# The pool of the expert tables' staging tiles moves from right behind h^T to the top of SBUF

## The chip, the cores and the metric

The kernel runs on one core of one Trainium2 chip. The metric is the device time of one execution in microseconds: the median of three runs is 1944.34 us (1943.15 to 1944.63). The profile shown below is of one further execution.

## The reference

256 tokens of width 1024 pass through two residual layers, all in float32. Layer 0 mixes the tokens with gated DeltaNet heads and block attention, layer 1 with latent attention. After each mixer stands the PEER feed-forward layer, which takes most of the time: 8 heads choose 16 of 16384 single-neuron experts for each token, and

```
act = gelu(einsum('td,ted->te', h, u[expert]))
out = einsum('te,ted->td', gates * act, v[expert])
```

Here `h` is the normalised and modulated activation, `u` and `v` are two tables of 16384 x 1024 in each layer.

## The kernel before

**No gather.** The kernel doesn't fetch the chosen experts. It multiplies h with the whole table u, weighs the result by a matrix of gates that is zero where an expert wasn't chosen, and multiplies that by the whole table v. Each table comes in 128 slabs of 128 experts (512 KB each) per layer.

**Two numbers for one.** A float32 value is split in a rounded part hi and a rest lo (`split`, line 131: ScalarE writes hi with a cast, VectorE writes lo with a subtraction). A product of two such values is three TensorE products: hi by hi, hi by lo, lo by hi.

**A matmul has two operands in SBUF.** The stationary one (128 x 128) is loaded into the array by an LDWEIGHTS, the moving one (256 or 512 columns) then streams through it. The profile shows the first as PEld, the second as PE, and names them in the order moving, stationary: `ps<-hT,hi` has hT as moving operand and hi as stationary one. Each matmul has its own LDWEIGHTS, which runs beside the matmul ahead of it.

**The stages of one layer's experts.** The u stage (`u_slab`, lines 619 to 628) loads a slab of u into `raw` (3 buffers), splits it into `hi` and `lo` (2 buffers each), and issues 24 matmuls of 256 columns: 16 of line 626 (8 k-tiles of hi as stationary operand, each with both parts of h^T moving) and 8 of line 628 (lo with the first part of h^T). Beside it VectorE selects the experts (`choose`) in the first half, and builds the gate matrix (`g_batch`, lines 639 to 653) in the second. The v stage (`v_pair`, line 783) loads a slab of v into the same `raw`, splits it into the same `hi` and `lo`, and issues 12 matmuls of 512 columns with hi or lo moving; the stationary operand is the weighted activation, split into `whi` and `wlo` of the pool `oh`. The last six slabs of a layer have lines of their own (736).

**Other products.** The projections (lines 135 to 137) go by weights that are loaded to `wraw` and split into `whi` and `wlo` of the pool `wp`, which lies at the right end of SBUF; the PEER queries (`queries`) are such products with h^T moving and the weights stationary, 48 of 256 columns for each of six groups in a layer. Line 323 (`two_tiles`) has weights moving and h^T stationary; these weights lie in several pools, and those of the first queries in `hi` and `lo` among others.

**What orders the work.** Tile pools are stacks that grow from the left or the right end of a partition's bytes. `hp` (h^T) and `st` (`raw`, `hi`, `lo`) are opened first and stay open to the end; the pools of the stages are opened and closed above them. All table and weight transfers are issued by SyncE, and wait there for a buffer.

Of the kernel before, what the change touches and what calls it, by code (L numbers as in the profile page):

```python
# [67 lines left out]
class Trunk:  # L68
# [222 lines left out]
    def tail(self, products, add, nxt, tmp):  # L291


        def run(g):
            for _ in g:
                pass
        run(products(0, 0))
        run(products(0, 1))
        run(add(0, 0))
        run(add(0, 1))  # L300
        nxt.norm(0)
        run(products(1, 0))
        p = products(1, 1)
        next(p)
        squares = add(1, 0)
        next(squares)
        nxt.turn(0)
        run(p)
        nxt.make(0, tmp, squares)
        run(add(1, 1))  # L310
# [1330 lines left out]
    def run(self, out):  # L1641
        nc = self.nc
        self.hp = self.ctx.enter_context(self.pool("h"))
        self.st = self.ctx.enter_context(self.pool("st"))
        right, late = ExitStack(), ExitStack()
        self.order = ExitStack()
        start = ExitStack()
# [243 lines left out]
```

## Time and profile before

| | |
|---|---|
| median of the runs | 1944.34 us |
| the profiled execution's own time | 1942.01 us |
| its span, first to last instruction | 1940.2 us |
| granted TensorE clock, mean share | 0.999 |
| TensorE busy | 1908.1 us (98%) |
| weight loads busy | 1753.0 us (90%) |
| VectorE busy | 1534.9 us (79%) |
| ScalarE busy | 952.7 us (49%) |
| the core's 16 DMA engines busy | 57.4% |

TensorE is busy almost throughout, so the time goes by what TensorE does and how fast. The busy share says nothing on that speed: matmuls overlap, and one that takes longer from start to start looks just as busy. So a matmul's pace is read from the starts of two matmuls and the count between them.

### The profile page before, as it was taken

Reading aid. Unit: us, or ns where it says so; the run is one execution under the profiler, and the core shown is the slowest. Engines: PE = TensorE matmul, PEld = TensorE weight load, DVE = VectorE, ACT = ScalarE, POOL = GpSimd, SP = SyncE. Lnnn points to the kernel's source line nnn. Section 1 sums busy time; section 2 is a strip of 40 time slices with the busy share of each in tenths; the row PEclk is TensorE's granted clock in tenths of the full one; section 3 lists DMA queues with packets and bytes.
Section 4 is the critical chain, followed back from the end, with each engine's and each line's share of the span. In section 5 each row is a group of like instructions: output and inputs, shape, how many; then the busy total and the mean of one; then the engine's idle time right before and its main releaser. Section 6 shows DMA issues by size and latency. Waiting matters only on the chain.

```text
span 1940.2 us, 36008 instructions
## 1 busy us (share of the span) xinstructions
PE 1908.1 (98%) x14368; PEld 1753.0 (90%) x14368; DVE 1534.9 (79%) x3265; ACT 952.7 (49%) x1309; POOL 49.9 (3%) x131
## 2 busy tenths in 40 slices
PE   6999999999999999999999999999999999999998
PEld 6999999999999888888889899999999988888886
DVE  7879699989977789877657668898777778985565
ACT  3866545454344444445546664545444444444453
POOL 7000000000000000000000000000000000000000
PEclk9999999999999999999999999999999999999999
DMA  7557485558645555589743454555545555556673
GB/s 319 177 172 250 187 275 179 185 187 291 229 164 167 172 175 174 178 286 331 229 129 115 163 218 169 183 187 178 171 164 169 168 174 175 173 176 204 192 224 106
DMA packets 97080, 376.67 MB, mean 194 GB/s; under 512 B 11920, under 2 KB 12176, under 8 KB 90256
## 3 DMA queue, kind: packets, MB, share of 16 engines
q1 hardware_dynamic: 96912, 374.37, 57.4%
q8 instruction: 112, 1.84, 0.4%
q14 instruction: 56, 0.46, 0.1%
HBM read 373.28 MB, written 1.05 MB: 193 GB/s over the span
## 4 chain that ended last, share of the span: by engine, by line
PE 88%; DVE 4%; DMA 3%; ACT 2%; issue 1%; SPq 0%; ACTq 0%; DVEq 0%
PE ps L783 31%; PE ps L626 26%; PE ps L628 13%; PE ps L649 3%; PE ps L135 3%; PE ps L136 3%; PE ps L137 3%; DMA raw<-in_v_dram 2%; PE ps L736 1%; PE ps L323 1%; DVE wlo L131 1%; PE ps L1207 1%; DMA wraw<-in_w_dram 1%; PE ps L946 1%; PE ps L456 1%
## 5 line engine op out<-in xcount | busy, mean ns | idle before, releaser
L131 ACT CAST hi<-raw 128x1024 fp32r<-128x1024 f32 x508 | 533.6, 1051 | 772.6 <-PE ps L626 385.4
L131 DVE TENSOR_TENSOR lo<-raw,hi 128x1024 fp32r<-128x1024 f32 x508 | 619.8, 1221 | 260.7 <-ACT hi L131 256.7
L626 PE MATMUL ps<-hT,hi 128*128 128x256 f32 x4096 | 538.3, 284 | 0.0
L626 PEld LDWEIGHTS ps<-hT,hi 128*128 128x128 f32 x4096 | 509.0, 192 | 0.0
L628 PE MATMUL ps<-hT,lo 128*128 128x256 f32 x2048 | 287.2, 283 | 0.0
L783 PE MATMUL ps<-hi,whi 128*128 128x512 f32 x976 | 266.4, 394 | 2.0 <-ACT hi L131 1.9
L628 PEld LDWEIGHTS ps<-hT,lo 128*128 128x128 f32 x2048 | 264.2, 192 | 0.0
L783 PE MATMUL ps<-hi,wlo 128*128 128x512 f32 x976 | 261.3, 389 | 0.0
L783 PE MATMUL ps<-lo,whi 128*128 128x512 f32 x976 | 261.2, 389 | 0.0
L783 PEld LDWEIGHTS ps<-hi,wlo 128*128 128x128 f32 x976 | 183.2, 188 | 38.8
L783 PEld LDWEIGHTS ps<-lo,whi 128*128 128x128 f32 x976 | 183.1, 188 | 38.9 <-DVE lo L131 0.2
L783 PEld LDWEIGHTS ps<-hi,whi 128*128 128x128 f32 x976 | 180.1, 188 | 39.3 <-ACT hi L131 4.5
L131 DVE TENSOR_TENSOR wlo<-wraw,whi 128x1024 fp32r<-128x1024 f32 (+1 forms) x84 | 98.7, 1200 | 41.0 <-ACT whi L131 41.0
L131 ACT CAST whi<-wraw 128x1024 fp32r<-128x1024 f32 (+1 forms) x84 | 83.7, 1031 | 30.7 <-PE ps L137 9.3
L645 DVE TENSOR_TENSOR ohG<-ohB,t 128x512 f16<-128x512 f16 x256 | 98.6, 416 | 0.0
L135 PE MATMUL ps<-hT,whi 128*128 128x256 f32 x288 | 84.0, 292 | 7.7 <-ACT hT L246 7.1
L639 DVE TENSOR_TENSOR ohA<-t,t 128x1024 f16<-128x1024 f16 x128 | 87.3, 682 | 0.0
L136 PE MATMUL ps<-hT,whi 128*128 128x256 f32 x288 | 82.1, 285 | 0.2 <-DVE hT L250 0.2
L137 PE MATMUL ps<-hT,wlo 128*128 128x256 f32 x288 | 82.2, 286 | 0.0
L649 PE MATMUL ps<-ohG,ohA 128*128 128x64 f16 x2048 | 78.6, 193 | 0.0
L649 PEld LDWEIGHTS <-ohA 128*128 128x128 f16 x2048 | 67.0, 97 | 12.1 <-issue 8.5
L353 DVE SCALAR_TENSOR_TENSOR t<-t 128x1024 f32<-128x1024 f32 x56 | 67.4, 1219 | 12.6 <-DMA t<-in_modT_dram 9.5
(480 smaller groups left out, 2254.6 us busy)
## 6 DMA issues: line engine op xcount, KB each, us to landing
raw<-in_uT_dram SPq DMA_DIRECT2D x256, 512.0 KB, 3.3
raw<-in_v_dram SPq DMA_DIRECT2D x256, 512.0 KB, 3.8
t<-in_modT_dram SPq DMA_DIRECT2D x56, 512.0 KB, 5.3
wraw<-in_w_dram SPq DMA_DIRECT2D x13, 1024.0 KB, 5.9
raw<-in_modT_dram SPq DMA_DIRECT2D x24, 512.0 KB, 4.4
wraw<-in_wq_dram SPq DMA_DIRECT2D x12, 1024.0 KB, 5.9
mw<-in_mod_dram SPq DMA_DIRECT2D x8, 1024.0 KB, 13.8
wraw<-in_w0start_dram SPq DMA_DIRECT2D x4, 1024.0 KB, 12.0
```

Source lines behind the costliest of these rows:

```text
L131: return self.nc.scalar.copy(hi, src), self.nc.vector.tensor_sub(lo, src, hi.bitcast(F32))
L135: mm(out, l[0], r[0], start=start, stop=False)
L136: mm(out, l[0], r[1], start=False, stop=False)
L137: mm(out, l[1], r[0], start=False, stop=stop)
L323: mm(ps[g][:, i], e.hT[:, s, k, sl], w[:, b, k, :], start=s + k + b == 0, stop=s == 1 and n == KD - 1)
L353: self.nc.vector.scalar_tensor_tensor(w, w, 1.0, row, op0=OP.mult, op1=OP.mult, accum_out=self.modc[layer][:, c:c + 1])
L626: mm(pair, hi[:, k], hT[:, s, k], start=k == 0 and s == 0, stop=False)
L628: mm(pair, lo[:, k], hT[:, 0, k], start=False, stop=k == KD - 1)
L639: nc.vector.tensor_tensor(A, self.iota_t[:, None].to_broadcast(full), pairs(0, full), op=OP.is_equal)
L645: nc.vector.tensor_tensor(B[:, j], b0, pairs(2 + j, part), op=OP.mult)
L649: nc.tensor.matmul(ps[:, t], A[:, t // 2, :, t % 2], B[:, j, t // 2, :, t % 2], start=j == 0, stop=j == 1)
L783: self.nc.tensor.matmul(acc[i][c], w[a][:, j, i * P:(i + 1) * P], v[b][:, c * 512:(c + 1) * 512], start=first and j + a + b == 0, stop=False)
```

## The change

One argument is added: the pool `st` is taken from the right end of SBUF.

```diff
         self.hp = self.ctx.enter_context(self.pool("h"))
-        self.st = self.ctx.enter_context(self.pool("st"))
+        self.st = self.ctx.enter_context(self.pool("st", side="right"))
         right, late = ExitStack(), ExitStack()
```

In the two programs as they are built every engine has the same instructions in the same order with the same waits. Only addresses differ. The pools behind `st` on the left move down by its 28672 bytes, those at the right end move down by as much to make room, and `st` itself moves up by 170304 bytes. The start of the tiles that the text speaks of, in bytes of a partition, with the remainder by 512:

| tile | before | rem. | after | rem. |
|---|---|---|---|---|
| hT (pool h) | 13984 | 160 | 13984 | 160 |
| raw (st), the first of 3 | 30368 | 160 | 200672 | 480 |
| lo (st) | 42656, 46752 | 160 | 212960, 217056 | 480 |
| hi (st) | 50848, 54944 | 160 | 221152, 225248 | 480 |
| whi, wlo of the v stage (oh), layer 0 | 84128 to 92320 | 160 | 55456 to 63648 | 160 |
| whi, wlo of the v stage (oh), layer 1 | 71840 to 80032 | 160 | 43168 to 51360 | 160 |
| wraw, whi, wlo of the projections (wp) | 163808 to 229344 | 480 | 135136 to 200672 | 480 |
| ckT, cqT, in layer 1's mixer | 67264, 71360 | 192 | 38592, 42688 | 192 |
| dead and qkT, in layer 0's mixer | 77472 on, 93856 | 160 | 48800 on, 65184 | 160 |

Slices within these tiles begin at multiples of 512 bytes from their start, so the remainder of a tile is that of each of its matmul operands.

## Rows read from the trace of the kernel before

**Rows 1.** The page: busy time by engine, and the chain by line.
```profile
PE 1908.1 (98%) x14368; PEld 1753.0 (90%) x14368; DVE 1534.9 (79%) x3265; ACT 952.7 (49%) x1309; POOL 49.9 (3%) x131
...
PE ps L783 31%; PE ps L626 26%; PE ps L628 13%; PE ps L649 3%; PE ps L135 3%; PE ps L136 3%; PE ps L137 3%; DMA raw<-in_v_dram 2%; PE ps L736 1%; PE ps L323 1%; DVE wlo L131 1%; PE ps L1207 1%; DMA wraw<-in_w_dram 1%; PE ps L946 1%; PE ps L456 1%
```
**Rows 2.** Stretches: start:end length, busy PE PEld DVE ACT POOL, PEclk, DMA, GB/s.
```profile
261.00:648.00 387.00, 387.00 (x3591) 385.71 (x3590) 338.01 (x861) 178.46 (x206) 1.53 (x1) 1.00 0.61 203
648.00:830.00 182.00, 182.00 (x1239) 149.88 (x1239) 156.60 (x268) 80.16 (x92) 0.00 (x0) 1.00 0.55 175
...
1175.00:1562.00 387.00, 387.00 (x3591) 385.71 (x3590) 314.99 (x805) 173.96 (x202) 1.53 (x1) 1.00 0.52 172
```
**Rows 3.** The chain in order of time: start us, us, what.
```profile
264.36 1.92 PE ps L626 x16
267.24 1.92 PE ps L626 x16
...
1744.07 113.47 PE ps L783 x500
```
**Rows 4.** Lines 626 and 628: count, ns min/median/max, first and last start.
```profile
L626 PEld LDWEIGHTS ps<-hT,hi x4096: 187/192/192, 261.2 to 1561.6; 128*128 128x128 f32 x196
L626 PE MATMUL ps<-hT,hi x4096: 278/283/365, 261.2 to 1561.7; 128*128 128x256 f32 x196
...
L628 PE MATMUL ps<-hT,lo x2048: 279/283/283, 263.2 to 1562.6; 128*128 128x256 f32 x187
```
**Rows 5.** Line 135 with h^T moving, the same view.
```profile
L135 PEld LDWEIGHTS ps<-hT,whi x288: 186/188/333, 22.6 to 1171.8; 128*128 128x128 f32 x144
L135 PE MATMUL ps<-hT,whi x288: 276/276/583, 22.6 to 1171.9; 128*128 128x256 f32 x144
```
**Rows 6.** Timeline of PE in two query groups: start us, us, instruction.
```profile
226.10 0.28 PE L136 MATMUL ps<-hT,whi 128*128 128x256 f32 x1
...
231.40 0.28 PE L136 MATMUL ps<-hT,whi 128*128 128x256 f32 x1
...
1160.81 0.28 PE L135 MATMUL ps<-hT,whi 128*128 128x256 f32 x1
...
1165.57 0.28 PE L135 MATMUL ps<-hT,whi 128*128 128x256 f32 x1
```
**Rows 7.** Line 323, view as in rows 4: moving operand in st, wp, ckT.
```profile
L323 PE MATMUL ps<-hi,hT x64: 276/283/387, 206.3 to 1133.6; 128*128 128x256 f32 x64
...
L323 PE MATMUL ps<-whi,hT x64: 278/279/386, 1019.9 to 1033.2; 128*128 128x256 f32 x64
...
L323 PE MATMUL ps<-ckT,hT x8: 277/278/281, 1121.1 to 1130.0; 128*128 128x256 f32 x8
```
**Rows 8.** Timeline of PE, products of 512 columns in the projections.
```profile
181.75 0.40 PE L136 MATMUL ps<-wlo,qkT 128*128 128x512 f32 x1
...
191.37 0.39 PE L136 MATMUL ps<-wlo,qkT 128*128 128x512 f32 x1
...
1102.73 0.40 PE L135 MATMUL ps<-whi,cqT 128*128 128x512 f32 x1
...
1104.60 0.40 PE L137 MATMUL ps<-whi,cqT 128*128 128x512 f32 x1
```
**Rows 9.** Stretches of layer 0's u stage, columns as in rows 2.
```profile
350.00:400.00 50.00, 50.00 (x419) 50.00 (x419) 47.54 (x217) 22.80 (x26) 0.00 (x0) 1.00 0.55 181
452.00:500.00 48.00, 48.00 (x504) 47.67 (x503) 47.42 (x88) 19.56 (x24) 0.00 (x0) 1.00 0.84 284
```
**Rows 10.** Groups by shape: busy, mean ns | idle before, releasers.
```profile
L131 DVE TENSOR_TENSOR lo<-raw,hi 128x1024 fp32r<-128x1024 f32 x508 | 619.8, 1221 | 260.7 <-ACT hi L131 256.7 <-PE ps L783 1.6
...
L131 DVE TENSOR_TENSOR wlo<-wraw,whi 128x1024 fp32r<-128x1024 f32 x80 | 96.2, 1225 | 41.0 <-ACT whi L131 41.0
```
**Rows 11.** DMA issues: form, count, KB each, median us to landing.
```profile
raw<-in_v_dram SPq DMA_DIRECT2D x256, 512.0 KB, 3.8
...
wraw<-in_w1out_dram SPq DMA_DIRECT2D x4, 1024.0 KB, 4.8
```

## The prediction

> **What bounds the kernel now.** I read the page first: TensorE is busy 98% of the span, and the chain that ended last runs through it: line 783 (v stage) 31%, lines 626 and 628 (u stage) 39% [rows 1]. [...] So an edit pays there only if it changes the pace of the matmuls or if another engine falls behind TensorE. The program's order and waits are unchanged, so the question is whether pace depends on where operands lie. The busy time can't say that. The start times can.
>
> The pace of the u stage: the 16 matmuls of line 626 begin at 264.36 and, one slab later, at 267.24, so 24 matmuls take 2.88 us, 120.0 ns each [rows 3]. Nearly all are alike: line 628 has a minimum of 279 and a median of 283 ns [rows 4]. The same form, h^T moving over 256 columns and a 128 x 128 weight tile standing, is found in the query groups. There 42 steps from 1160.81 to 1165.57 take 4.76 us, 113.3 ns each, and 45 steps from 226.10 to 231.40 take 5.30 us, 117.8 ns each [rows 6]. By start times, 9 of the 12 groups (6 a layer) have the first pace and 3 the second; none has 120. The single durations agree: a load of 192 ns and a matmul of 283 in the u stage [rows 4], 188 and 276 at line 135 [rows 5].
>
> What differs? Not the moving tile (h^T in both), the columns or the clock. By the table of addresses, the u stage's two operands have the same remainder by 512 (160 and 160), those of the query groups don't (160 and 480). Line 323 separates this from the loop: one loop, h^T standing, weights moving from several pools. From hi (remainder 160, equal to h^T's) the median is 283, from whi (480) 279, from ckT (192) 278 [rows 7]. ckT starts at byte 67264 and hi at 50848, h^T at 13984, so ckT isn't much farther from h^T than hi is: I take it that the low address bits count, equal ones costing about 7 ns a matmul, and not the distance. Whether 512 is the period or 128 or 256 the rows can't tell; 160 and 480 differ by all three.
>
> **The change, part by part.** Only `st` changes its remainder, from 160 to 480. All other moved tiles go down by 28672 bytes, 56 times 512.
>
> U stage. Matmuls: 4096 + 2048 = 6144 [rows 4], all from equal remainders to unequal ones, 160 moving against 480 standing, exactly the query groups' case. Value taken: the groups' mean, (9 x 113.3 + 3 x 117.8) / 12 = 114.4 ns, 5.6 less than 120.0: 34.4 us. Bounds: 6.7 x 6144 = 41.2 if all go at 113.3, 2.2 x 6144 = 13.5 if all go at 117.8, and 0 if the addresses aren't the reason.
>
> V stage. Here hi and lo move and whi and wlo stand. Now both have remainder 160; later 480 against 160. Matmuls: 122 slabs x 12 x 2 layers = 2928. Pace now: 500 in 113.47 us, 226.9 ns [rows 3]. Nearest row for 480 against 160 at 512 columns: 42 steps from 181.75 to 191.37, 9.62 us, 229.0 ns [rows 8]. So this stage loses: 2.1 x 2928 = 6.1 us. Bounds: 8 steps from 1102.73 to 1104.60, 1.87 us, 233.8 ns (480 against 192) [rows 8], which would be +6.9 x 2928 = 20.2 us; below nothing, the 256-column products' fall of 6.7 ns, a gain of 19.6 us. No 512-column row shows that, so I take the nearest one.
>
> What is late next. In layer 0's u stage VectorE is busy 338.01 of 387.00 us [rows 2], but 47.54 of 50 in one stretch and 47.42 of 48 in another [rows 9]. At 114.4 ns the first needs 47.7 us of TensorE, just enough cover. In the second, VectorE lets no more than 0.6 us go of some 2. With what is lost around single slabs I take 3 us off the gain, between 0 and 8; the 8 is half of layer 0's 17.2. Layer 1 has 314.99 of 387 [rows 2] and loses nothing.
>
> Splits and transfers. A VectorE subtraction in `st` takes 1221 ns, one in `wp`, which ends where `st` will end, 1225 [rows 10]: 4 ns, off the chain. A slab lands in 3.8 us for 512 KB, a weight tile at the right end in 4.8 for 1024 KB [rows 11], so nothing there is slower by the byte; counted as 0, and the casts too. The 64 matmuls of line 323 with hi moving gain 4 ns each, 0.3 us, counted as 0.
>
> Sum: -34.4 + 6.1 + 3 = -25.3 us. The profiled execution took 1942.0 us, so 1916.7; the median of the runs is 2.3 above that execution, which gives **1919.0 us**.
>
> [...]
>
> **The rivals.**
> *The addresses don't matter.* The 120.0 could come from the u loop's order (16 of hi, then 8 of lo), and the 113.3 from the projections' order of three. For it: both paces, 113.3 and 117.8, occur in one piece of code, so something besides the address sets the pace. Against it: line 323 has one order and three durations. The changed kernel would then be the old one: 1944.3 us. [...]
> *Slower: the v stage pays more than the u stage gets.* V's matmuls go to 233.8 ns, +20.2 us, while u only reaches 117.8, -13.5: +6.7, or 1951 us. With the u pace unchanged and v at 229.0 it is +6.1, or 1950. It decides once v's loss per matmul exceeds 2.1 times u's gain per matmul (6144 / 2928). For it: both 512-column stretches with unequal remainders are above 226.9 [rows 8]. Against it: the row nearest in operands asks for 2.1 ns only.
> *VectorE takes over.* If layer 0's u stage gains nothing, -17.2 + 6.1 = -11.1, or 1933 us. For it, 47.42 of 48; against it, 338 of 387 for the whole.
>
> **How the numbers follow.** Forecast 0.74, VectorE 0.04, no effect 0.13, slower 0.09. The forecast's own range: u all at 113.3 with v unchanged, -41.2 + 3 = -38, 1906; u all at 117.8 with v at 229.0, -7.4, 1937. To hold 8 in 10 I go up to 1945, which takes in the case without effect, and down to 1904, for no loss at VectorE: 1904 to 1945. Bounds for a measurable change are 0.2%, 3.9 us: faster 0.78 (forecast and VectorE), same 0.13, slower 0.09.
>
> **What would show it.** Right: lines 626 and 628 with medians of about 188 (load) and 276 to 281 (matmul), a slab every 2.72 to 2.83 us, both u stages some 370 us long; line 783 at about 229 ns from start to start; subtractions at 1221 and landings at 3.8 unchanged. Wrong: u still at 2.88 us a slab (no effect of addresses); v over 232 ns; or TensorE waiting for `lo` through layer 0's u stage, which would put the bound on VectorE.

## The result and the profile after

The changed kernel takes 1918.45 us (median of 4 executions, 1916.8 to 1922.05), the kernel before 1944.49 beside it: ratio 0.987, 95% interval 0.9853 to 0.9887, so 26.0 us less. The forecast was 1919.0.

The profiled execution took 1922.05 us, the slowest of the four, while that of the kernel before (1942.01) lies under all its other ones (1943.15 to 1944.75). The two traces are therefore only 19.9 us apart (spans of 1940.2 and 1920.3), and it is these 19.9 us that can be laid out stage by stage.

The page after, busy time by engine and the chain by engine; it answers to [rows 1]:

```profile
PE 1881.9 (98%) x14368; PEld 1717.7 (89%) x14368; DVE 1533.5 (80%) x3265; ACT 951.6 (50%) x1309; POOL 49.6 (3%) x131
...
PE 78%; DVE 10%; DMA 7%; ACT 3%; issue 2%; SPq 0%; ACTq 0%; DVEq 0%
```

TensorE still is busy 98% of the span, with 26.2 us less of it and as many instructions. The stages are read from the first and last start of a line, one layer at a time. Lines 626 (u) and 783 (v) of the kernel before, layer 0 then layer 1 (count, ns min/median/max, first and last start):

```profile
L626 PE MATMUL ps<-hT,hi x2048: 278/283/365, 261.2 to 647.5; 128*128 128x256 f32 x187
...
L626 PE MATMUL ps<-hT,hi x2048: 278/283/365, 1175.5 to 1561.7; 128*128 128x256 f32 x187
...
L783 PE MATMUL ps<-hi,whi x488: 388/389/504, 648.5 to 999.2; 128*128 128x512 f32 x163
...
L783 PE MATMUL ps<-hi,whi x488: 388/389/499, 1562.8 to 1911.7; 128*128 128x512 f32 x163
```

The same rows of the changed kernel:

```profile
L626 PE MATMUL ps<-hT,hi x2048: 276/276/384, 261.5 to 635.6; 128*128 128x256 f32 x187
...
L626 PE MATMUL ps<-hT,hi x2048: 276/276/369, 1170.4 to 1538.9; 128*128 128x256 f32 x187
...
L783 PE MATMUL ps<-hi,whi x488: 387/392/505, 636.6 to 993.8; 128*128 128x512 f32 x163
...
L783 PE MATMUL ps<-hi,whi x488: 388/392/505, 1539.9 to 1891.5; 128*128 128x512 f32 x163
```

| stage, first to last start | before | after | difference |
|---|---|---|---|
| u, layer 0 | 386.3 | 374.1 | -12.2 |
| u, layer 1 | 386.2 | 368.5 | -17.7 |
| v, layer 0 | 350.7 | 357.2 | +6.5 |
| v, layer 1 | 348.9 | 351.6 | +2.7 |

Their sum is -20.7 us; what lies ahead, between and behind is 0.8 longer. The two u stages, alike before, differ by 5.6 us after.

The pace shows in the chain of the changed kernel in order of time (start us, us, what), as in [rows 3]:

```profile
328.32 1.81 PE ps L626 x16
331.05 1.81 PE ps L626 x16
...
1722.41 103.56 PE ps L783 x452
```

A slab of 24 matmuls comes every 2.73 us, 113.8 ns each; it was 2.88 and 120.0. In the v stage 103.56 / 452 is 229.1 ns against 226.9. The single durations of lines 626 and 323 after (they answer to [rows 4] and [rows 7]):

```profile
L626 PEld LDWEIGHTS ps<-hT,hi x4096: 186/188/192, 261.4 to 1538.8; 128*128 128x128 f32 x196
L626 PE MATMUL ps<-hT,hi x4096: 276/276/384, 261.5 to 1538.9; 128*128 128x256 f32 x196
```

```profile
L323 PE MATMUL ps<-hi,hT x64: 276/279/392, 206.5 to 1128.6; 128*128 128x256 f32 x64
...
L323 PE MATMUL ps<-dead,hT x48: 277/280/289, 206.8 to 219.6; 128*128 128x256 f32 x48
...
L323 PE MATMUL ps<-ckT,hT x8: 280/280/284, 1116.1 to 1124.9; 128*128 128x256 f32 x8
```

Load 188 and matmul 276 ns are those of line 135 in [rows 5]. VectorE's subtraction is as before (1221 ns in [rows 10]), and a v slab lands in 3.7 us (3.8 in [rows 11]):

```profile
L131 DVE TENSOR_TENSOR lo<-raw,hi 128x1024 fp32r<-128x1024 f32 x508 | 619.4, 1221 | 239.6 <-ACT hi L131 235.7 <-issue 0.2
```

```profile
raw<-in_v_dram SPq DMA_DIRECT2D x256, 512.0 KB, 3.7
```

### The profile page after: what moved, and what is told of

Read it like the earlier page. It is cut to its first block, busy times and chain, and to the rows that moved or that the text cites. A ratio compares the mean times of both kernels' runs of the same rounds, so it can differ in the third digit from the quotient of the medians.

```text
span 1920.3 us, 36008 instructions
## 1 busy us (share of the span) xinstructions
PE 1881.9 (98%) x14368; PEld 1717.7 (89%) x14368; DVE 1533.5 (80%) x3265; ACT 951.6 (50%) x1309; POOL 49.6 (3%) x131
## 3 DMA queue, kind: packets, MB, share of 16 engines
HBM read 373.28 MB, written 1.05 MB: 195 GB/s over the span
## 4 chain that ended last, share of the span: by engine, by line
PE 78%; DVE 10%; DMA 7%; ACT 3%; issue 2%; SPq 0%; ACTq 0%; DVEq 0%
PE ps L783 28%; PE ps L626 21%; PE ps L628 10%; PE ps L649 3%; PE ps L135 3%; PE ps L137 3%; DVE lo L131 3%; PE ps L136 3%; DMA raw<-in_v_dram 3%; DMA t<-in_modT_dram 2%; PE ps L736 1%; PE ps L323 1%; DVE wlo L131 1%; PE ps L1207 1%; ACT hi L131 1%
## 5 line engine op out<-in xcount | busy, mean ns | idle before, releaser
L131 DVE TENSOR_TENSOR lo<-raw,hi 128x1024 fp32r<-128x1024 f32 x508 | 619.4, 1221 | 239.6 <-ACT hi L131 235.7
L626 PE MATMUL ps<-hT,hi 128*128 128x256 f32 x4096 | 514.3, 278 | 1.7 <-ACT hi L131 1.7
L626 PEld LDWEIGHTS ps<-hT,hi 128*128 128x128 f32 x4096 | 485.8, 188 | 1.9 <-ACT hi L131 1.9
L628 PE MATMUL ps<-hT,lo 128*128 128x256 f32 x2048 | 276.3, 277 | 1.5 <-DVE lo L131 1.4
L628 PEld LDWEIGHTS ps<-hT,lo 128*128 128x128 f32 x2048 | 252.4, 188 | 2.9 <-DVE lo L131 2.7
L649 PEld LDWEIGHTS <-ohA 128*128 128x128 f16 x2048 | 67.3, 97 | 12.2 <-issue 8.9
```

The costliest lines, as they stand in the source:

```text
L131: return self.nc.scalar.copy(hi, src), self.nc.vector.tensor_sub(lo, src, hi.bitcast(F32))
L626: mm(pair, hi[:, k], hT[:, s, k], start=k == 0 and s == 0, stop=False)
L628: mm(pair, lo[:, k], hT[:, 0, k], start=False, stop=k == KD - 1)
L649: nc.tensor.matmul(ps[:, t], A[:, t // 2, :, t % 2], B[:, j, t // 2, :, t % 2], start=j == 0, stop=j == 1)
```

## The experiments

Theory: the pace of TensorE follows the low bits of the moving operand's address against those of the standing one. Main rival: it is the place, `st` far from h^T or in the upper part of SBUF. All kernels but one compute the same, with the same instructions; they differ in unused bytes ahead of a pool or tile, with further ones behind it so that the other tiles keep their remainders. Each ratio is to the kernel before on the same chip, whose median was 1944.49 us beside the changed kernel and 1945.6 to 1946.2 us beside the others.

In the table the distance is the standing operand's remainder less the moving one's, by 256. The paces are the mean steps between matmul starts over both layers, in the one trace of each kernel; steps over 130 ns (u) or 250 ns (v) are left out, since those hold waits or other work.

| kernel | st at | u: distance, ns | v: distance, ns | time, us | ratio, interval |
|---|---|---|---|---|---|
| before | left, 160 | 0, 120.0 | 0, 227.3 | | 1 |
| after | top, 480 | 64, 114.0 | 192, 229.1 | 1918.45 | 0.987 (0.9853 to 0.9887) |
| top_equal | top, 160 | 0, 120.0 | 0, 227.3 | 1945.07 | 0.9997 (0.9987 to 1.0007) |
| left_unequal | left, 480 | 64, 114.0 | 192, 229.0 | 1919.61 | 0.9867 (0.985 to 0.9883) |
| h_too (h^T at 480) | top, 480 | 0, 120.0 | 192, 229.0 | 1953.26 | 1.0041 (1.0028 to 1.0053) |
| d256 | top, 416 | 0, 120.0 | 0, 227.3 | 1945.62 | 0.9997 (0.9988 to 1.0007) |
| d128 | top, 288 | 128, 118.9 | 128, 233.0 | 1953.45 | 1.004 (1.0025 to 1.0055) |
| d32 | top, 192 | 32, 118.3 | 224, 233.3 | 1950.76 | 1.0017 (1.0006 to 1.0027) |
| d192 | top, 96 | 192, 117.0 | 64, 233.3 | 1940.8 | 0.9982 (0.997 to 0.9993) |
| v_equal | top, 480 | 64, 115.7 | 0, 227.3 | 1924.39 | 0.9893 (0.9877 to 0.991) |
| oh_early | top, 480 | 64, 116.0 | 192, 229.2 | 1931.19 | 0.9927 (0.9911 to 0.9944) |
| v_only | top, 480 | 64, 113.9 | 0, 227.2 | 1915.9 | 0.9839 (0.9823 to 0.9854) |
| d96_v | top, 256 | 96, 118.2 | 0, 227.3 | 1936.57 | 0.9949 (0.993 to 0.9969) |
| light | top, 480 | 64, 114.0 | 192, 229.0 | 1919.22 | 0.9864 (0.9848 to 0.9881) |

**Place or low bits.** First the move without the new remainder, then the new remainder without the move (both edits against the changed kernel).

```diff
+        self.t(self.ctx.enter_context(self.pool("gap", side="right")), [P, 80])
         self.st = self.ctx.enter_context(self.pool("st", side="right"))
+        self.t(self.ctx.enter_context(self.pool("gap2", side="right")), [P, 48])
```

> The pool st stays at the top of SBUF, but 320 bytes lower, so that hi and lo have h^T's remainder by 512 again (160 and 160); 192 further bytes below it keep every other tile's remainder. Theory of the low address bits: lines 626 and 628 back at 120.0 ns from start to start (load 192, matmul 283), line 783 back at 227.2; time 1940 to 1945 us. Rival, it is the place (the distance from h^T, or the upper part of SBUF): 114.1 and 229.1 ns as in the changed kernel; 1917 to 1922 us.

```diff
-        self.st = self.ctx.enter_context(self.pool("st", side="right"))
+        self.t(self.ctx.enter_context(self.pool("gap")), [P, 80])
+        self.st = self.ctx.enter_context(self.pool("st"))
+        self.t(self.ctx.enter_context(self.pool("gap2")), [P, 48])
```

> The pool st lies behind h^T as before the change, but 320 bytes further, so that hi and lo have remainder 480 against h^T's 160; 192 further bytes behind it keep the other tiles' remainders. Theory of the low address bits: u stage at 114.1 ns, line 783 at 229.1, so the time of the changed kernel without any move to the top: 1917 to 1922 us. Rival, it is the place: 120.0 and 227.2 ns; 1942 to 1946 us.

The low bits carry all of it: the move alone brings nothing (0.9997), the 320 bytes alone bring the whole gain (0.9867). One slab of top_equal in the chain, at 1.92 us for 16 as before:

```profile
331.40 1.92 PE ps L626 x16
333.32 0.96 PE ps L628 x8
```

Line 626 of left_unequal, with the durations of the changed kernel:

```profile
L626 PE MATMUL ps<-hT,hi x4096: 276/276/387, 260.4 to 1535.1; 128*128 128x256 f32 x196
```

**Equality or a good value.** h^T is moved by 320 bytes too.

```diff
+        self.t(self.ctx.enter_context(self.pool("gaph")), [P, 80])
         self.hp = self.ctx.enter_context(self.pool("h"))
+        self.t(self.ctx.enter_context(self.pool("gaph2")), [P, 48])
```

> The changed kernel with the pool of h^T 320 bytes further and 192 bytes behind it: h^T has remainder 480, hi and lo 480; whi and wlo of the v stage keep 160. Theory that equal remainders count and not the particular value: u stage back at 120.0 ns with line 783 still at 229.1, so 1947 to 1952 us, slower than before. Rival, 480 is a good remainder for a standing tile and 160 a bad one: u stage at 114.1, 1917 to 1922 us.

Equality: 480 against 480 is at 120.0 ns again, and the v stage's loss is left (229.0 ns). The time, 1953.26 us, is 1.3 over the expected range, which left out one thing that the trace shows: with h^T at 480 the query groups' operands are equal too, since their weights lie at 480. All 12 groups now have a mean step of 119.7 to 120.0 ns, where the kernel before has 113.4 to 117.8, an estimated 3 us for their 576 matmuls. So the effect also appears in matmuls that have no operand in `st`. Line 626 and a v piece of h_too (112.72 / 492 = 229.1 ns), and between them line 135, which had a median of 276 ns in [rows 5]:

```profile
L626 PE MATMUL ps<-hT,hi x4096: 278/283/366, 264.1 to 1569.6; 128*128 128x256 f32 x196
```

```profile
L135 PE MATMUL ps<-hT,whi x288: 277/283/582, 22.6 to 1179.7; 128*128 128x256 f32 x144
```

```profile
1753.22 112.72 PE ps L783 x492
```

**The period, and what lies within it.** The edit is top_equal's, with gaps of 64, 192, 288 and 384 bytes.

> The pool st at the top with remainder 416 (64 bytes lower than in the changed kernel), which is 256 from h^T's 160 and from that of whi and wlo. If the period of the effect is 512: u stage near 114 ns, 1917 to 1922 us. If it is 256, 128 or 64: u stage at 120.0 ns as for equal remainders, line 783 at 227.2, 1940 to 1945 us. If it is the place and no remainder: 114.1 and 229.1, 1917 to 1922 us.

> The pool st at the top with remainder 288: 128 from h^T's 160 and from that of whi and wlo, in the other direction than 480 (192 from it). If the period is 256 (416 was as slow as equal, 480 not): u stage faster than 120.0 ns, at 113 to 118, time 1915 to 1935 us. If the period is 128: 120.0 and 227.2 ns, 1942 to 1948 us.

> The pool st at the top with remainder 192, 32 from h^T's 160. If any difference inside the period gives the faster pace: u stage at 113 to 118 ns, 1915 to 1935 us. If operands that fall into the same 64 or 128 bytes behave as equal ones: 120.0 ns, 1942 to 1948 us.

> The pool st at the top with remainder 96, 64 below h^T's 160 instead of 64 above it (by 256). Theory that only the size of the distance counts: u stage at 113 to 114.5 ns, line 783 at 229, so the changed kernel's 1917 to 1922 us. Rival, the sign counts (standing ahead of moving is another case than behind it, so what is good for the u stage is bad for the v stage): u stage at 117 to 120 ns, 1930 to 1950 us.

At 256 bytes (d256) u and v have the paces of equal operands, 120.0 and 227.3 ns, at 128 (d128) they don't, 118.9 and 233.0: the period is 256, as far as the distances tried tell. Within it no simple rule came out. For the u stage 32, 96 and 128 bring 1 to 2 ns only (118.3, 118.2 and 118.9), 64 brings 6 (114.0). The expectation of d192 that only the size of the distance counts fell: 64 below h^T (192 by 256) gives 117.0 ns in the u stage where 64 above gives 114.0, and in the v stage 64 gives 233.3 and 192 gives 229.1. The 117.0 is a mix, though: d192 starts both u stages at 113.3 ns, the pace of distance 64, and goes over to 117.8 after 20 and 23 slabs for good. Its traced execution is also one of three at 1945.66 to 1946.38 us; the other seven took 1939.12 to 1940.88, so there the mix may be another. All unequal distances tried cost the v stage something (229.0 to 233.3 ns against 227.3). These pieces show an equal pair, d256 (227.0 ns), and an unequal one, d32 (233.5):

```profile
1750.91 99.87 PE ps L783 x440
```

```profile
1750.32 173.70 PE ps L783 x744
```

The times expected of d32 and d128 (under 1935 us if the u stage got faster) left the v stage out and were missed. The two kernels are the forecast's slower rival come true: with d128 the u stage gets 1.1 x 6144 = 6.8 us and the v stage pays 5.7 x 2928 = 16.7, 9.9 more in all; measured are 7.6 (1953.45 against 1945.83). The times of top_equal and d256 lie 0.1 and 0.6 us over their ranges.

**A version with both stages at their best, and what spoilt the first try.** With the whole pool `oh` moved:

```diff
         oh = left.enter_context(self.pool(f"oh{layer}"))
         a1 = left.enter_context(self.pool(f"act1_{layer}"))
         act1 = self.act_tiles(a1)
+        self.t(oh, [P, 80])
```

> The changed kernel with 320 bytes ahead of the tiles of the pool oh, so that whi and wlo of the v stage have remainder 480, like hi and lo, while h^T against hi and lo stays unequal. Theory of the low address bits, with equal ones better at 512 columns: u stage unchanged at 114.1 ns, line 783 from 229.1 to 227.2; 1.9 x 2928 = 5.6 us less than the changed kernel, 1912 to 1914 us. Rival, the v stage's pace comes from the place of hi and lo at the top or from VectorE and the transfers: line 783 stays at 229.1, 1917 to 1922 us.

The v stage did what was expected (227.3 ns). The time did not fall (1924.39 us), because the second half of both u stages, where line 649 runs between the slabs, slowed down (0.94 us for eight matmuls of line 628 at 1402.49 us, 0.91 in the changed kernel at 1403.89). The next two runs part the tiles that had moved together: v_only puts the 320 bytes ahead of whi and wlo alone, oh_early ahead of ohA, ohB and ohG alone (and of the index tile that VectorE builds them from).

```diff
         accs = [[self.ps("o") for _ in range(2)] for _ in range(TT)]
+        self.t(oh, [P, 80])
...
+        self.t(oh, [P, 48])
         mods, ready = after()
```

> The changed kernel, in which only whi and wlo of the v stage go to remainder 480 (320 bytes ahead of them, 192 behind); the tiles of line 649 and the gelu's results keep 160, unlike in the run v_equal. Theory, the v stage's pace follows the remainders and the u stage's second half was spoilt in v_equal by the other tiles that moved with the pool oh: u stage at 113 to 114 ns in both halves, line 783 at 227.2, so 5.6 us under the changed kernel: 1911 to 1915 us. Rival, whi and wlo themselves or chance spoilt the u stage in v_equal (117.8 ns in the second half of the stage): 1922 to 1926 us as there.

> The changed kernel in which only the tiles of line 649 (ohA, ohB, ohG) go from remainder 160 to 480; whi, wlo and the gelu's results keep 160. Theory, the short matmuls of line 649 decide in which of its two paces the u stage goes on: the second half of both u stages at 117 to 118 ns instead of 113.4 as in v_equal, line 783 at 229.1, so 8 us over the changed kernel: 1925 to 1929 us. Rival, the gelu's result tiles did it in v_equal (they had moved too): u stage at 113.4 in the second half, 1917 to 1921 us.

The tiles of line 649 did it: 1931.19 us in oh_early, 1915.9 in v_only. In v_equal and oh_early the second half is at the slower pace, some 117.8 ns, in both layers, in the changed kernel, left_unequal, v_only and light mostly at the faster one, some 113.4, in both. The pace depends on how much of line 649 ran just ahead. In layer 1's second half of the changed kernel, the second slab behind 16 of its matmuls is at the faster pace, 1.81 us for 16 of line 626, and the second slab behind 32, two batches in a row, at the slower one:

```profile
1437.62 0.50 PE ps L649 x16
...
1440.92 1.81 PE ps L626 x16
...
1443.64 0.98 PE ps L649 x32
...
1447.53 1.89 PE ps L626 x16
```

In oh_early, with h^T, hi and lo at the same addresses, it is the other way round:

```profile
1444.55 0.50 PE ps L649 x16
...
1447.96 1.89 PE ps L626 x16
...
1450.79 0.98 PE ps L649 x32
...
1454.60 1.81 PE ps L626 x16
```

Behind 16 matmuls of line 649 the changed kernel, left_unequal, v_only and light go on at the faster pace in 27 or 28 of a layer's 28 places, v_equal and oh_early at the slower one in 24 to 27. The time of oh_early is 2.2 us over its range; its layer 0 also has a slower first half (115.5 against 114.2 ns, 1.3 x 1536 = 2.0 us), which the next lines show.

So for one pair of remainders the u stage has two paces, some 113.4 and 117.8 ns, and stays in one for many slabs (up to 33 in the changed kernel). In these traces a change from one slab to the next stands at an interruption: a step of over 200 ns, or matmuls of line 609 or 649 in between. In layer 1 all six kernels with distance 64 change at the same four of the first 61 slabs (23, 30, 53 and 60, counted from 0), so these changes are not chance. The addresses alone don't settle it: oh_early has the changed kernel's operand addresses all through layer 0's first half, yet it began that stage in the second pace (a slab every 2.83 us from 266.54 on), in which it stayed for some 30 slabs:

```profile
266.54 1.88 PE ps L626 x16
268.43 0.94 PE ps L628 x8
269.37 1.89 PE ps L626 x16
```

In the changed kernel the second pace follows on one disturbed piece (1.05 us for eight matmuls):

```profile
404.84 1.81 PE ps L626 x16
406.65 1.05 PE ps L628 x8
407.70 1.88 PE ps L626 x16
```

v_only beats the kernel before clearly. Against the changed kernel it was not timed directly: its ratio is 0.0031 lower, 6 us, where the v stage's 1.9 x 2928 = 5.6 were expected; the intervals (0.9823 to 0.9854 and 0.9853 to 0.9887) just overlap, so the step from one to the other is likely, but not shown by the times. Its 1915.9 us is 0.9 over the expected range. Its v piece (102.58 / 452 = 226.9 ns):

```profile
1714.34 102.58 PE ps L785 x452
```

The last run looked for a better distance for the u stage and found none (118.2 ns and 1936.57 us at 96):

> A search for a version better than v_only (1915.9 us): st at remainder 256, 96 from h^T's 160, and whi and wlo of the v stage at 256 too, as equal as in v_only. The v stage is expected at 227.2 ns by all theories. For the u stage the runs so far have 120.0 ns at distance 0, 118.3 at 32, 113.4 (second pace 117.8) at 64 and 119.0 at 128. If 64 is the bottom of a valley between 32 and 128: 116 to 118.5 ns at 96, 6144 times 2 to 4.5 ns over v_only, 1928 to 1943 us. If the pace falls on beyond 64: under 113.4 ns, under 1912 us.

**VectorE in layer 0's u stage.** The 32 modulation tiles are cut:

```diff
-                    self.mod_tile(layer, c, w, row)
+                    self.mod_tile(layer, c, *(x[:, :8 if (layer, p) in ((0, 5), (1, 0), (1, 1), (1, 2)) else D] for x in (w, row)))
```

> The changed kernel in which the 32 modulation tiles (line 353) that VectorE works off in layer 0's u stage are summed over 8 of their 1024 columns; the rest of that sum is left out, their transfers stay. Theory, VectorE holds TensorE back in layer 0's u stage: that stage (first to last slab) goes from 372.4 us to layer 1's 366.8 or a little less, so 4 to 6 us under the changed kernel: 1912 to 1915 us, with no TensorE wait for lo. Rival, the transfers are late there (DMA share 0.82 between 450 and 500 us): the stage stays at 371 to 373, the time at 1917 to 1921 us.

Weight loads of the changed kernel in layer 0's u stage (columns: busy us, mean ns, idle before us and releaser):

```profile
L626 PEld LDWEIGHTS ps<-hT,hi 128*128 128x128 f32 x2048 | 242.9, 188 | 1.9 <-ACT hi L131 1.9
L628 PEld LDWEIGHTS ps<-hT,lo 128*128 128x128 f32 x1020 | 125.8, 188 | 2.8 <-DVE lo L131 2.7
```

and of light, with the first and last start of line 626 in that stage:

```profile
L626 PEld LDWEIGHTS ps<-hT,hi 128*128 128x128 f32 x2048 | 242.9, 188 | 1.4 <-ACT hi L131 1.3
L628 PEld LDWEIGHTS ps<-hT,lo 128*128 128x128 f32 x1024 | 126.2, 188 | 0.1
```

```profile
L626 PE MATMUL ps<-hT,hi x2048: 276/276/385, 264.5 to 634.6; 128*128 128x256 f32 x187
```

The wait for lo is gone, and the stage takes 370.1 us in place of 374.1; layer 1's takes 368.5. (The expectation counts from slab to slab, 1.7 less for each stage.) So by these two traces VectorE costs 4.0 of the 5.6 us; the stage takes 373.1 to 374.6 us in the three kernels that have this work and the same paces (the changed kernel, left_unequal and v_only). The remaining 1.6 is above all a wait for the cast of hi (1.3 us idle in light), which stands behind a transfer of the conditioning vector, as the chain of light has it:

```profile
429.44 6.89 DMA t<-in_cond_dram
...
436.40 0.10 ACT L349
436.50 1.19 issue
437.69 1.06 ACT t L349
438.75 0.94 ACT hi L131
```

The time, 1919.22 us, missed the expected 1912 to 1915: four executions lie between 1914.84 and 1919.79, and 4 us can't be told from the changed kernel's 1916.8 to 1922.05. Its stage began 3.0 us later in the profiled execution for reasons ahead of it (between the kernels' traces that start varies from 259.9 to 264.5).

## Why the prediction was right, by its steps

- **The cause, low address bits and not the distance: right, and shown** by top_equal, left_unequal and h_too together (120.0, 114.0 and 120.0 ns in the u stage). What the text left open, 128, 256 or 512, is 256 by d256 and d128 (120.0 and 118.9). One of its arguments was weaker than it looked. Line 323's three medians [rows 7] were read as three pairs of remainders, but after the change `dead,hT`, still 160 against 160, goes from 283 to 280 ns, and `ckT,hT`, with its pair unchanged, from 278 to 280. So in a loop that mixes operands a single duration doesn't go by its own pair alone. The comparison that carried was that of start times in long runs of one pair. The line of `dead` before:

```profile
L323 PE MATMUL ps<-dead,hT x48: 279/283/287, 206.5 to 219.3; 128*128 128x256 f32 x48
```

- **The u stage, -34.4 us: right.** Measured 120.0 - 114.0 = 6.0 ns, or 36.9 us over 6144 matmuls, against 5.6 forecast. To take a mean over two paces was right: both occur in the stage, 221 of the 256 slabs of the changed kernel's trace at the faster one. Their shares were borrowed from the query groups, 9 to 3, and that these came so close is partly luck: with the same remainders for h^T, hi and lo, v_equal has 115.7 ns and oh_early 116.0.
- **VectorE late in layer 0, +3 us (0 to 8): right in place and sign, too small.** The stage lost 5.6 us against layer 1's, 4.0 of it to VectorE by the traces of the changed kernel and light. The two windows of [rows 9] show busy time; the cast's wait behind a transfer isn't in them.
- **The v stage, +6.1 us: the pace was right, the stages lost more.** 1.8 ns x 2928 = 5.3 us; the nearest row [rows 8], 229.0 ns, is what came (229.1). Its operands are at distance 192, like those of the changed v stage. The row of the upper bound, 233.8 ns, is at 224, and d32, which puts the v stage at 224, has 233.3; so the rows of before already held both of these v paces. The stages are 9.2 us longer, and the difference lies in layer 0's waits: at the same pace that stage's length differs between the kernels here (352.5 to 357.0 us from first to last matmul at 227.4 ns), so the 4 us beyond the pace can't be put down to the change.
- **The sum.** -25.3 forecast, -26.0 by the medians, -19.9 between two traces. The four executions of the changed kernel spread over 5.3 us, and by the traces a larger gain of u (36.9 for 34.4) stands against larger losses of VectorE and v; that the forecast lies 0.6 us from the median is in part luck.
- **By what means: not shown.** The pace is 120.0 ns in top_equal and 114.0 in the changed kernel, with nothing changed but 320 bytes of address. So it depends on the addresses of TensorE's own two operands, one against the other; what makes it so no run here tells.
- **The rivals.** "The addresses don't matter" is ruled out by top_equal against left_unequal (120.0 and 114.0 ns, ratios 0.9997 and 0.9867); what spoke for it, that something besides the address also moves the pace, held (the two paces, 113.4 and 117.8 ns). "Slower, v pays more" did not happen here, but does at distances 32 and 128 (ratios 1.0017 and 1.004). Its weighing of v against u was sound, and the changed kernel's distance of 64 for u (192 for v) is, of the unequal ones tried, the one at which u gains most (6.0 ns) and v loses least (1.8).

## What to carry to other kernels

Where TensorE is the bound, measure the pace from start to start for each pair of operands, and compare forms that differ only in address: a few hundred unused bytes ahead of one pool gave 1.3% here (left_unequal), and a pool that comes to lie at another remainder can cost 0.4% (d128). Which remainder is good differs between the two stages here (equal for v's 512 columns, 227.3 ns; 64 apart for u's 256, 114.0), so each stage wants its own padding. The two also differ in which operand lies in `st`; no run parts this from the columns. When a tile moves, list what moves with it: the tiles of short matmuls between two slabs changed the pace of the long ones (116.0 ns in oh_early against 114.0).

## What was not expected of the hardware

- The pace of a chain of 256-column matmuls depends on the operands' distance by 256 bytes: 120.0 ns at 0, 118.3 at 32, 114.0 at 64, 118.2 at 96, 118.9 at 128, 117.0 at 192 (means of the u stages; at 64 and 192 the pace changes within the stage, and at 128 it is 120.0 at 330 us, 1.92 us for 16 matmuls, and some 118 at 1400 us, 0.94 us for eight). For 512 columns it is 227.3 at 0, 233.3 at 64, 233.0 at 128, 229.1 at 192, 233.3 at 224: equal operands are the slowest of those tried there and the fastest here.
- At 64 and 192 there are two paces, some 113.4 and 117.8 ns. The changed kernel keeps one for up to 33 slabs, and each of its 18 changes stands at a step of over 200 ns or at matmuls of line 609 or 649. Which one follows line 649 depends on how many of its matmuls ran in between, 16 or 32 (1.81 and 1.89 us for 16 of line 626 in the changed kernel, the reverse in oh_early), and on the remainder of their tiles (160 in the changed kernel, 480 in oh_early). It also differed between two traces with the same operand addresses (layer 0's first half, changed kernel and oh_early). What sets it stays open.
